# Preparing the recurrence's operands inside the projections instead of inside the recurrence

## The chip, the cores and the metric

The kernel runs on one core of a Trainium2 chip. The metric is the device time of one execution in microseconds (us). The engines are TensorE (PE in the profile, with PEld for its weight loads), VectorE (DVE), ScalarE (ACT), GpSimd (POOL) and SyncE (SP, which here only issues DMAs). Each engine works through its own queue in order and waits at an instruction whose inputs are not there yet.

## What is computed

One step of a two-layer decoder trunk in float32, for 1024 prompt tokens and for 64 sample tokens (8 sequences of 8) that share the weights. Layer 0 mixes with a convolution, layer 1 with RWKV-7; behind each mixer come cross-attention and a squared-ReLU MLP. The change touches the RWKV mixer alone:

```
xr, xw, xk, xv, xa, xg = (h + xx * mix[i] for i in range(6))        # xx = previous token - h
r, k, v = xr @ w_r, xk @ w_k, xv @ w_v
decay = exp(-exp(-softplus(-(w0 + tanh(xw @ w1) @ w2)) - 0.5))
a = sigmoid(a0 + (xa @ a1) @ a2);   g = sigmoid(xg @ g1) @ g2
kk = k * k_k;  kk = kk / max(norm(kk per head), eps);   k = k * (1 + (a - 1) * k_a)
for each token t, per head:                                         # state s is 64 x 64
    s = s * decay_t + (s @ -kk_t) (kk_t * a_t)^T + v_t k_t^T;   y_t = s @ r_t
y = groupnorm(y) * lnx_g + lnx_b + sum(r * k * r_k per head) * v
out = (y * g) @ w_o
```

The kernel works the loop over tokens in chunks of 64: inside a chunk it is a handful of matrix products and the inversion of a triangular matrix, and from chunk to chunk only the state goes on.

## The kernel before, in words

**Two streams.** The tokens are cut in two parts. Part A holds 512 prompt tokens, part B the other 512 and the 64 samples. Each part is a generator of work (`first()` and `second()`), and `pace` draws from both by a running estimate of their cost, so that in the program A's work stands between B's. A framework then schedules every engine's queue from its own model of durations. A's state goes into B, so B's recurrence comes after A's. The order in time is: A's projections beside B's first MLP, A's recurrence beside the end of that MLP and the start of B's projections, B's projections beside A's output product, B's recurrence beside A's second attention and MLP, and at the end B's second attention and MLP.

**Matrix products.** A weight tile `raw` (128 x 1024, 512 KB) comes by DMA, ScalarE rounds it to a high part (L96), VectorE makes the low part (L97), and `prod` does three matmuls for each piece (L142 to L144). `B_d<-u,wt` in a row is B's MLP, `A_d` and `B_d` are the streams' PSUM banks.

**Projections** (`projections`, from L729). `project(slot, ...)` makes r, k and v for eight row blocks m of 128 channels and two token tiles. Beside it run the small products: `hidden` makes the narrow side of the low-rank products and `lora` the wide one. All results go by a DMA from ScalarE's queue (`store`, L847) to six slots of `scr` in HBM. The last of them, `lora("a")`, stands behind the products of v.

**Shared splits.** The 24 weight tiles of r, k and v serve both parts. A writes the low part of each to `low` in HBM (`put`, L103), and B's `load` fetches it (L125) instead of making it.

**Recurrence** (`scan`, from L1088). For each chunk of 64 tokens three generators run side by side: `prep` of a chunk, `inverse` of the one before and `rest` (state, output, `finish`) of the one before that. `prep` loads all eight row blocks of the chunk as 128 x 512 tiles and makes from them `ar` (kk and r times the decay so far), `bk` (minus kk * a and k over the decay), the bonus `bon` and the norms `d32`: seven VectorE instructions of 512 columns (L1166 to L1258) and four small ones for the norms (L1212), three on ScalarE (L1168 to L1179), and six on GpSimd (L1189 to L1202). `finish` normalises the output with five GpSimd instructions of 512 columns (L1467 to L1471). A's recurrence has 8 chunks, B's has 8 and one of the samples: 17 in all.

## Time and profile before

| | us |
|---|---|
| three runs | 3832.77, 3834.26, 3837.16 |
| median | 3834.26 |
| the profiled execution | 3837.42 |
| its span, first to last instruction | 3835.7 |
| TensorE busy in the span | 3623.9 (94%) |
| VectorE, ScalarE, GpSimd busy | 2351.6, 1610.0, 660.7 |
| mean granted TensorE clock | 0.955 of 2.4 GHz |

The page says where the time is: TensorE is busy nearly throughout, at full clock in most slices. The exceptions are the convolution at the start, a stretch around 1900 us, and 2300 to 2800 us, where both the busy share and the granted clock fall. TensorE's busy time counts matmuls that overlap, and one at the lower of the two clock levels (1.2 GHz) is busy for longer, so busy time and clock are to be read together. All times below are counted from the start of the span.

### The profile page before, as it was taken

The numbers are of one execution on the slowest core, as the hardware profiler recorded it, in microseconds if no ns is written. First come the engines' busy times: TensorE is split into PE (matmuls) and PEld (weight loads), VectorE is DVE, ScalarE is ACT, GpSimd is POOL, SyncE is SP. The second block draws the span as 40 slices with busy tenths as digits, with TensorE's granted clock in tenths as the row PEclk, the third lists the DMA queues.
The fourth block names the chain that finished last, engine by engine and source line by source line (L and its number), as shares of the span: only waits on it lengthen the run. The fifth ranks groups of instructions, "written<-read, shape, count | busy, mean of one in ns | idle before, by whom it ended". The sixth has DMA issues, their size and how long they took to land.

```text
span 3835.7 us, 75763 instructions
## 1 busy us (share of the span) xinstructions
PE 3623.9 (94%) x30906; PEld 3369.6 (88%) x30906; DVE 2351.6 (61%) x4479; ACT 1610.0 (42%) x3190; POOL 660.7 (17%) x704
## 2 busy tenths in 40 slices
...
GB/s 226 132 53 129 80 67 106 102 114 170 153 90 83 126 151 152 159 138 112 85 88 109 232 254 146 111 93 70 54 113 120 114 120 197 121 72 83 83 83 64
DMA packets 333004, 456.03 MB, mean 119 GB/s; under 512 B 155248, under 2 KB 247664, under 8 KB 332656
## 3 DMA queue, kind: packets, MB, share of 16 engines
...
q14 instruction: 105, 0.86, 0.1%
...
## 4 chain that ended last, share of the span: by engine, by line
PE 77%; DVE 11%; ACT 4%; DMA 4%; issue 2%; POOL 1%; SPq 1%; ACTq 0%; DVEq 0%; POOLq 0%
PE B_d L142 11%; PE B_d L144 11%; PE B_d L143 11%; PE A_d L142 10%; PE A_d L143 9%; PE A_d L144 9%; PE A_d L362 3%; PE B_d L362 2%; DMA scr<-t_st 1%; SPq L1151 1%; PE A_hd L810 1%; PE A_d L442 1%; PE B_sa L608 1%; DVE wt L97 1%; PE B_sa L610 1%
## 5 line engine op out<-in xcount | busy, mean ns | idle before, releaser
L97 DVE TENSOR_TENSOR wt<-raw,wt 128x1024 fp32r<-128x1024 f32 x447 | 567.3, 1272 | 476.9 <-ACT wt L96 473.0
L96 ACT CAST wt<-raw 128x1024 fp32r<-128x1024 f32 x488 | 508.5, 1047 | 502.2 <-PE B_d L144 268.6
L142 PE MATMUL B_d<-hAB,wt 128*128 128x288 f32 (+1 forms) x2240 | 673.6, 303 | 15.4 <-ACT hAB L96 6.3
L143 PE MATMUL B_d<-hBB,wt 128*128 128x288 f32 (+1 forms) x2240 | 668.5, 299 | 1.2 <-DVE hBB L97 1.1
L144 PE MATMUL B_d<-hAB,wt 128*128 128x288 f32 (+1 forms) x2240 | 666.2, 298 | 0.3 <-DVE wt L97 0.3
L142 PE MATMUL A_d<-hAA,wt 128*128 128x256 f32 x2240 | 639.1, 288 | 15.0 <-ACT hAA L96 13.6
L143 PE MATMUL A_d<-hBA,wt 128*128 128x256 f32 x2240 | 642.4, 288 | 3.4 <-DVE hBA L97 3.4
L144 PE MATMUL A_d<-hAA,wt 128*128 128x256 f32 x2240 | 632.8, 285 | 2.5 <-POOL wt L97 2.2
L142 PEld LDWEIGHTS A_d<-hAA,wt 128*128 128x128 f32 x2240 | 429.0, 192 | 25.1 <-ACT hAA L96 16.8
L142 PEld LDWEIGHTS B_d<-hAB,wt 128*128 128x128 f32 x2240 | 425.4, 191 | 24.5 <-ACT hAB L96 7.5
L143 PEld LDWEIGHTS A_d<-hBA,wt 128*128 128x128 f32 x2240 | 430.2, 192 | 14.3 <-DVE hBA L97 5.6
L144 PEld LDWEIGHTS A_d<-hAA,wt 128*128 128x128 f32 x2240 | 428.6, 192 | 7.3 <-POOL wt L97 2.6
L143 PEld LDWEIGHTS B_d<-hBB,wt 128*128 128x128 f32 x2240 | 427.2, 191 | 6.5 <-DVE hBB L97 3.7
L711 POOL TENSOR_TENSOR t_sg<-t_ev 128x256 f32<-128x256 f32 (+1 forms) x256 | 185.5, 725 | 1418.2 <-ACT t_ev L709 1329.3
L144 PEld LDWEIGHTS B_d<-hAB,wt 128*128 128x128 f32 x2240 | 426.1, 190 | 2.3 <-issue 0.7
L142 PE MATMUL B_d<-u,wt 128*128 128x288 f32 x1024 | 307.1, 301 | 0.0
L144 PE MATMUL B_d<-u,wt 128*128 128x288 f32 x1024 | 303.3, 299 | 0.0
L143 PE MATMUL B_d<-u,wt 128*128 128x288 f32 x1024 | 303.3, 298 | 0.0
L143 PE MATMUL A_d<-u,wt 128*128 128x256 f32 x1024 | 288.2, 282 | 0.0
L144 PE MATMUL A_d<-u,wt 128*128 128x256 f32 x1024 | 288.2, 282 | 0.0
L142 PE MATMUL A_d<-u,wt 128*128 128x256 f32 x1024 | 287.4, 282 | 0.0
L97 DVE TENSOR_TENSOR u<-t_sg,u 128x256 fp32r<-128x256 f32 (+1 forms) x256 | 130.4, 510 | 149.9 <-ACT u L96 149.6
(401 smaller groups left out, 7068.8 us busy)
## 6 DMA issues: line engine op xcount, KB each, us to landing
raw<-in_mlp_up_dram SPq DMA_DIRECT2D x128, 512.0 KB, 3.6
raw<-in_mlp_dn_dram SPq DMA_DIRECT2D x128, 512.0 KB, 3.6
raw<-in_rw_w_dram SPq DMA_DIRECT2D x64, 512.0 KB, 4.2
ld<-scr SPq DMA_DIRECT2D x136, 128.0 KB, 3.2
wf<-in_w_in_dram SPq DMA_DIRECT2D x32, 512.0 KB, 4.0
raw<-in_xa_w_q_dram SPq DMA_DIRECT2D x32, 512.0 KB, 3.6
raw<-in_xa_w_o_dram SPq DMA_DIRECT2D x32, 512.0 KB, 3.6
raw<-in_ck_dram SPq DMA_DIRECT2D x32, 512.0 KB, 3.6
```

The source lines that it names most:

```text
L96: self.nc.scalar.copy(hi, src)
L97: (engine or self.nc.vector).tensor_tensor(lo, src, hi.bitcast(F32), SUB)
L142: self.nc.tensor.matmul(out, lhsT=wh, rhs=mh, start=(i == 0), stop=False)
L143: self.nc.tensor.matmul(out, lhsT=wh, rhs=ml, start=False, stop=False)
L144: self.nc.tensor.matmul(out, lhsT=wl, rhs=mh, start=False, stop=(i == last))
L362: nc.tensor.matmul(ps[:, :n], lhsT=wt[:, 0, k * P:k * P + P], rhs=h[:, k, t0:t0 + n], start=(k == 0), stop=(k == NC8 - 1))
L442: nc.tensor.matmul(ps[hs], lhsT=dg[:, q, h], rhs=two[h][:, 2 * q:2 * q + 512], start=(q == 0), stop=(q == pairs - 1))
L608: nc.tensor.matmul(out[:, h2], lhsT=wt.rearrange("p i t -> p (i t)"), rhs=moving[:, 0], start=start, stop=stop)
L610: nc.tensor.matmul(out[:64, h2], lhsT=wt[:, 0], rhs=moving[:, 1], start=False, stop=False)
L711: nc.gpsimd.tensor_mul(sg[:, :n], r[:, :n], r[:, :n])
L810: nc.tensor.matmul(ps[:, :n], lhsT=w1[:, m:m + P], rhs=hc[:, :n], start=(c == 0), stop=(c == NC8 - 1))
L1151: nc.sync.dma_start(out=dst[..., m * 64:m * 64 + 64], in_=scr[part][m][:, slots, t0:t0 + 64])
```

## The change

**A stage between projections and recurrence.** A new generator `stage(m, c0)` loads the six slots of one row block m for a pair of chunks (128 tokens; B also has a piece of 64 sample tokens), makes in place what `prep` made, and writes all six to `tls` in HBM. Its tiles `ld` (3 buffers in A, 2 in B), `kk`, `t1` and `ones` (one buffer each) live with the projections. It has 6 instructions on ScalarE, 9 on VectorE, 3 on GpSimd, 5 matmuls (four of them one column wide) and two DMAs. The part of `finish` that needs no output is made here too (bonus, bias and gate in slot v; scale times gate in slot g). There are 32 stages in A and 40 in B.

**Where it runs.** `project` of v draws one row block's stages after each of its six groups of the last token tile; the stages of the last two row blocks come after the projections. `hidden("a")` moves to the products of r and `lora("a")` to those of v, since a stage needs all six slots. The hidden tile that w and a shared becomes two.

**The recurrence** loads `ar` and `bk` ready from `tls`, copies the norms (one VectorE instruction of 16 columns) and does `finish` with three GpSimd instructions in place of five.

**The splits.** `low`, `put` and the `share` path go: B makes its 24 low parts itself.

The diff, cut to its core:

```diff
-weights = s.weights([(a["rw_w"][i, m], 1024, P, None, None, low[i][m]) for i in range(3) for m in range(NC8)])
+weights = s.weights([(a["rw_w"][i, m], 1024, P) for i in range(3) for m in range(NC8)])
...
+def stage(m, c0):
+    n, l, e, rs, at = (64, DSEQ, tail, ...) if c0 == 8 else (half, 64, ones, rst, slice(c0, c0 + 2))
+    ts = slice(64 * c0, 64 * c0 + n)
+    ld = hp.tile([P, 6, half], F32, tag="ld", name="ld", bufs=3 - part)
+    nc.sync.dma_start(out=ld[:, :, :n], in_=scr[part][m][:, :, ts])
+    w, r, ag, k, v, g = (ld[:, i, :n] for i in range(6))
+    kk, t1 = (hp.tile([P, half], F32, tag=x, name=x)[:, :n] for x in ("kk", "t1"))
+    nc.scalar.activation(kk, k, AF.Copy, scale=col("k_k", m))
+    nc.scalar.activation(t1, k, AF.Square, scale=col("k_k", m))
+    ps = s.bank()
+    ... nc.tensor.matmul(ps[hs, i:i + 1], lhsT=t1[hs, 64 * i:64 * i + 64], rhs=bones[hs, hs][:, :1], ...)
+    nc.vector.tensor_scalar_max(sums[part][:, m, c0:c0 + n // 64], ps[:, :n // 64], L2_MIN)
+    nc.vector.tensor_tensor_scan(out=w, data0=rs, data1=w, initial=0.0, op0=MUL, op1=ADD)
+    nc.scalar.activation(e[:, :, 1:], by(w, l), AF.Exp, scale=-DECAY)
+    nc.scalar.activation(w, w, AF.Exp, scale=DECAY)
+    nc.scalar.activation(t1, ag, AF.Identity, scale=col("k_a", m), bias=less[:, m:m + 1])
+    nc.vector.scalar_tensor_tensor(out=ag, in0=kk, scalar=-1.0, in1=ag, op0=MUL, op1=MUL)
+    nc.vector.scalar_tensor_tensor(out=t1, in0=t1, scalar=1.0, in1=k, op0=ADD, op1=MUL)
+    nc.gpsimd.tensor_tensor(ag, ag, w, MUL)
+    nc.vector.tensor_tensor(k, t1, w, MUL)
+    nc.vector.scalar_tensor_tensor(out=t1, in0=r, scalar=col("r_k", m), in1=t1, op0=MUL, op1=MUL)
+    nc.gpsimd.tensor_copy(ends[part][:, m, at], e[:, :, l])
+    nc.gpsimd.tensor_tensor(by(r, l), by(r, l), e[:, :, 1:], MUL)
+    nc.vector.tensor_tensor(by(w, l), by(kk, l), e[:, :, :l], MUL)
+    ps = s.bank()
+    nc.tensor.matmul(ps[:, :n], lhsT=bones, rhs=t1, start=True, stop=True)
+    nc.vector.tensor_tensor(v, v, ps[:, :n], MUL)
+    nc.vector.scalar_tensor_tensor(out=v, in0=v, scalar=col("lnx_b", m), in1=g, op0=ADD, op1=MUL)
+    nc.scalar.activation(g, g, AF.Copy, scale=col("lnx_g", m))
+    nc.sync.dma_start(out=tls[part][m][:, :, ts], in_=ld[:, :, :n])
...
+                if slot == 2 and tt == tiles[-1]:
+                    for _ in range(1 + 3 * len(pieces)):
+                        yield next(tiles_of, 0)
...
-yield from project(2, None, hidden(4, "a", [AF.Copy]), lora("gh", 5))
-s.put()
-yield from lora("a", 4)
+yield from project(2, None, lora("a", 2), lora("gh", 5))
+yield from tiles_of
...
-        L = ws
-        nc.vector.tensor_tensor_scan(out=L, data0=masks["rst"], data1=ws, initial=0.0, op0=MUL, op1=ADD)
...
+        load(ld, chunk, slice(0, 4))
+        ar, bk = ld[:, :, :2], ld[:, :, 2:]
...
-        nc.gpsimd.tensor_tensor(v3(y), v3(y), bvec("lnx_g"), MUL)
-        nc.gpsimd.tensor_tensor(v3(y), v3(y), bvec("lnx_b"), ADD)
-        nc.gpsimd.tensor_add(y, y, w["bon"])
-        nc.gpsimd.tensor_mul(y, y, gg)
+        nc.gpsimd.tensor_mul(v3(y), v3(y), gb[:, :, 1])
+        nc.gpsimd.tensor_add(v3(y), v3(y), gb[:, :, 0])
```

Three places of the engines' queues show the move. Line numbers of the kernel after differ a little: its products are L126 to L128 and its recurrence's lines stand two or three lower or higher.

**TensorE, between A's projections and its recurrence.** Before, B's MLP (`B_d<-u`) stands between and around the first matmuls of the recurrence (L1208, L1381):

```order
L143 MATMUL B_d<-u,wt 128x288
L1208 MATMUL p_pp<-c_bones,w 128x2 x4
L144 MATMUL B_d<-u,wt 128x288
L142 MATMUL B_d<-u,wt 128x288
L143 MATMUL B_d<-u,wt 128x288
L144 MATMUL B_d<-u,wt 128x288
L143 MATMUL B_d<-u,wt 128x288
L144 MATMUL B_d<-u,wt 128x288
L1381 MATMUL p_pz<-S,ar 64x64 x16
```

After, the last stages of A (L887 the norms, L906 the bonus) follow each other; eight such pairs stand ahead of these rows, and `hAB` behind them is the first product of B's projections:

```order
L887 MATMUL A_d<-c_bones,t_18462 64x1 x4
L906 MATMUL A_d<-t_18462,c_bones 128x128
L887 MATMUL A_d<-c_bones,t_18528 64x1 x4
L906 MATMUL A_d<-t_18528,c_bones 128x128
L887 MATMUL A_d<-c_bones,t_18558 64x1 x4
L906 MATMUL A_d<-t_18558,c_bones 128x128
L887 MATMUL A_d<-c_bones,t_18588 64x1 x4
L906 MATMUL A_d<-t_18588,c_bones 128x128
L1226 MATMUL p_pp<-ld 128x128 x2
L1379 MATMUL p_pz<-S,ld 64x64 x2
L126 MATMUL B_d<-hAB,wt 128x288 x2
```

B's MLP has ended ahead of A's last stages, and nothing of B stands between them.

**VectorE, at the start of B's projections** (`rest` is their first instruction). Before, it stands in the middle of A's recurrence, here between its lines for the inversion (`M`, `td`, `T`), the state `S` and the output `y`; `xB` is B's residual:

```order
L1313 STREAM_TRANSPOSE td<-M_20121 128x16x32
L1407 TENSOR_TENSOR S<-p_pz,S 128x512
L1322 STREAM_TRANSPOSE T_20125<-td 128x256
L1408 TENSOR_TENSOR S<-S,pcs 128x512
L725 TENSOR_TENSOR xB_169<-xB_169,B_d 128x288
L769 TENSOR_SCALAR rest<-vec 128x48
L1456 SCALAR_TENSOR_TENSOR y<-p_pz,y 128x512
L1228 TENSOR_TENSOR Aak<-p_pp,c_strict_p 64x4x64
```

After, it stands one row behind A's last stage (L889 to L909 are a stage's lines), and A's recurrence begins with it:

```order
L889 TENSOR_SCALAR sums_105<-A_d 128x2
L896 SCALAR_TENSOR_TENSOR ld<-kk,ld 128x128
L897 SCALAR_TENSOR_TENSOR t_18588<-t_18588,ld 128x128
L899 TENSOR_TENSOR ld<-t_18588,ld 128x128
L900 SCALAR_TENSOR_TENSOR t_18588<-ld,vec,t_18588 128x128
L903 TENSOR_TENSOR ld<-kk,ones 128x128
L907 TENSOR_TENSOR ld<-ld,A_d 128x128
L909 SCALAR_TENSOR_TENSOR ld<-ld,vec 128x128
L1274 STREAM_TRANSPOSE dt<-d_18650 128x32
L756 TENSOR_SCALAR rest<-vec 128x48
```

So B's norm, which stood beside A's recurrence, now stands ahead of A's last stages, and B's mixing behind them.

**TensorE, A's second attention and MLP** (L558, L546 after: transposed softmax tiles). Before, the attention stands among the matmuls of B's recurrence:

```order
L1400 MATMUL p_half<-Aq,UV 64x64 x8
L1406 MATMUL p_pz<-UV,BK 64x64
L558 MATMUL A_d<-c_ident,e 128x128 x4
L1455 MATMUL p_pz<-y,c_bones 128x512
L142 MATMUL A_d<-pr,wt 128x256
```

After, it stands among B's stages, and B's recurrence stands among A's MLP (`A_d<-u`), here some 1600 rows later:

```order
L887 MATMUL B_d<-c_bones,t_27047 64x1 x2
L906 MATMUL B_d<-t_27047,c_bones 128x64
L546 MATMUL A_d<-c_ident,e 128x128 x4
L887 MATMUL B_d<-c_bones,t_27075 64x1 x4
L126 MATMUL A_d<-pr,wt 128x256
...
L1325 MATMUL p_half<-T_30500,dgz 32x16 x13
L128 MATMUL A_d<-u,wt 128x256
L126 MATMUL A_d<-u,wt 128x256
L1237 MATMUL p_pp<-c_ident,v 128x128 x4
```

## Rows read from the trace of the kernel before

**Rows 1.** Busy time by stage (engine busy us, count), granted clock, DMA share, GB/s:
```profile
core 0: us, PE busy (x) PEld busy (x) DVE busy (x) ACT busy (x) POOL busy (x), PEclk, DMA share, GB/s
1305.00:1734.00 429.00, 428.77 (x3300) 425.17 (x3299) 206.19 (x401) 198.74 (x431) 29.66 (x46) 1.00 0.49 153
1734.00:2140.00 406.00, 364.94 (x4759) 313.71 (x4759) 320.54 (x709) 225.01 (x448) 125.07 (x113) 0.90 0.38 105
2140.00:2391.00 251.00, 232.16 (x1599) 217.94 (x1598) 103.62 (x230) 125.37 (x275) 2.92 (x9) 0.95 0.70 218
2391.00:2865.00 474.00, 429.08 (x5517) 362.05 (x5516) 367.67 (x753) 226.25 (x453) 163.87 (x129) 0.88 0.31 81
2865.00:3366.00 501.00, 500.08 (x4103) 498.11 (x4102) 273.38 (x449) 207.91 (x370) 96.15 (x110) 1.00 0.43 136
```
**Rows 2.** The same view, single stretches of 100 us:
```profile
300.00:400.00 100.00, 95.48 (x564) 80.00 (x565) 96.16 (x166) 31.92 (x63) 7.62 (x12) 0.95 0.40 125
400.00:500.00 100.00, 96.52 (x569) 75.70 (x568) 96.31 (x154) 26.30 (x61) 15.41 (x10) 1.00 0.27 80
1800.00:1900.00 100.00, 91.77 (x1341) 79.54 (x1341) 77.18 (x163) 51.73 (x103) 36.42 (x33) 0.92 0.30 72
1900.00:2000.00 100.00, 80.98 (x1149) 65.39 (x1149) 89.69 (x227) 52.91 (x111) 34.65 (x35) 0.76 0.35 92
2000.00:2100.00 100.00, 94.97 (x1387) 80.10 (x1386) 72.68 (x159) 59.84 (x119) 24.33 (x20) 0.93 0.37 110
2600.00:2700.00 100.00, 97.28 (x1436) 82.86 (x1436) 83.03 (x164) 50.59 (x95) 35.02 (x27) 0.93 0.32 81
```
**Rows 3.** Chain of waits, 1880 to 2020 us, its shares by line:
```profile
by line: DVE xB L738 8.4%; DVE hBB L97 5.5%; DVE M L1304 4.7%; DVE t_dl L783 4.7%; issue 4.6%; DVE ld L1171 3.9%; SPq L1151 3.7%; PE B_d L142 3.6%; PE B_d L144 3.3%; PE B_d L143 3.3%; DVE hc L783 2.8%; DVE w L1192 2.5%; DVE Aak L1228 2.4%; 
```
**Rows 4.** VectorE groups of the recurrence, 1734 to 2140 us (busy us, mean ns):
```profile
L1171 DVE TENSOR_TENSOR_SCAN ld<-rst,ld 128x512 f32<-128x512 f32 x8 | 12.3, 1532 | 0.0
L1192 DVE SCALAR_TENSOR_TENSOR w<-ld,vec 128x512 f32<-128x512 f32 x8 | 8.2, 1029 | 0.0
L1194 DVE SCALAR_TENSOR_TENSOR ld<-w,ld 128x512 f32<-128x512 f32 x8 | 7.7, 964 | 0.0
L1197 DVE SCALAR_TENSOR_TENSOR w<-w,ld 128x512 f32<-128x512 f32 x8 | 6.4, 804 | 0.0
L1166 DVE TENSOR_TENSOR w<-ld,vec 128x512 f32<-128x512 f32 x8 | 5.6, 699 | 7.3 <-DMA gg<-scr 3.0 <-DMA v<-scr 2.5 <-issue 1.8
L1203 DVE TENSOR_TENSOR w<-w 128x512 f32<-128x512 f32 x8 | 5.5, 682 | 0.2 <-PE p_pp L1208 0.2
L1258 DVE TENSOR_TENSOR bon<-v,p_pp 128x512 f32<-128x512 f32 x8 | 5.4, 680 | 5.3 <-PE p_pp L1256 5.3
L1212 DVE TENSOR_SCALAR d<-p_pp 64x8 f32<-64x8 f32 x32 | 5.2, 163 | 0.8 <-PE p_pp L1208 0.5
```
**Rows 5.** Single lines, whole run: duration min/median/max in ns:
```profile
L786 DVE SCALAR_TENSOR_TENSOR t_dl<-before,vec,t_dl x24: 267/278/1286, 1995.2 to 2229.2; 128x64 f32<-128x64 f32 x24
L841 DVE TENSOR_TENSOR w<-raw,w x48: 283/290/420, 1337.9 to 2366.7; 128x128 fp32r<-128x128 f32 x48
L836 ACT CAST w<-raw x64: 280/294/309, 1336.7 to 2366.2; 128x128 fp32r<-128x128 f32 x48, 96x128 fp32r<-96x128 f32 x16
L1171 DVE TENSOR_TENSOR_SCAN ld<-rst,ld x17: 1191/1223/2290, 1743.9 to 2740.3; 128x512 f32<-128x512 f32 x17
```
**Rows 6.** Costliest groups of the page: the split of one weight tile:
```profile
L97 DVE TENSOR_TENSOR wt<-raw,wt 128x1024 fp32r<-128x1024 f32 x447 | 567.3, 1272 | 476.9 <-ACT wt L96 473.0
```
**Rows 7.** ScalarE group of a table load, 1734 to 2140 us:
```profile
L1463 ACT ACT_TABLE_LOAD x8 | 10.3, 1283 | 0.1
```
**Rows 8.** DMA issues: count, KB each, median us from issue to landing:
```profile
ld<-scr SPq DMA_DIRECT2D x136, 128.0 KB, 3.2
low<-wt SPq DMA_DIRECT2D x24, 512.0 KB, 3.0
wt<-low SPq DMA_DIRECT2D x24, 512.0 KB, 4.6
```
**Rows 9.** TensorE groups of the recurrence, 1734 to 2140 us:
```profile
L1208 PE MATMUL p_pp<-c_bones,w 128*128 128x2 f32 x64 | 10.7, 286 | 0.0
L1256 PE MATMUL p_pp<-w,c_bones 128*128 128x512 f32 x16 | 12.7, 886 | 0.0
L1381 PE MATMUL p_pz<-S,ar 64*64 64x64 f32 x256 | 12.8, 235 | 0.7 <-ACT rs L1463 0.7
L1245 PE MATMUL p_pp<-c_ident,bk 128*128 128x128 f32 x64 | 11.6, 318 | 5.5 <-DVE Aq L1229 5.1 <-ACT UV L1237 0.2
```

154 lines of the change are left out of this document (58 added, 96 removed).

## The prediction

> **What bounds the kernel now.** I read the page first: TensorE is busy 94% of the span, so time can only come from where it stands still or runs at the lower clock. The view by stages [rows 1] shows where that is. I call lost time the span less TensorE's busy time, plus the span times what the clock lacks to 1. A's projections (1305 to 1734 us) lose nothing: 428.77 busy of 429 at clock 1.00. A's recurrence (1734 to 2140) loses 41 + 0.10 x 406 = 82 us. B's projections (2140 to 2391) lose 19 + 0.05 x 251 = 31. B's recurrence (2391 to 2865) loses 45 + 0.12 x 474 = 102. Behind it nothing is lost again. The sum is 215 us, and the stages hold 324 + 220 + 372 = 916 us of TensorE's work beside it. Idle time at the lower clock is counted twice here, so 215 is a little high.
>
> What goes with the loss is VectorE's load. Per us of TensorE's work VectorE is busy 0.48 in A's projections, and 0.99 in both recurrences (320.54 / 324 and 367.67 / 372). Single stretches [rows 2] give the scale: at 0.83 (2000 to 2100) 12 us of 100 are lost, at 0.92 (1800 to 1900 and 2600 to 2700) 16 and 10, at 1.57 (1900 to 2000) 43. The worst stretch is B's norm and mixing beside A's recurrence; its chain of waits [rows 3] is led by VectorE lines of both. But 300 to 500 us, in the convolution, has VectorE at 96% and loses only 3.5 to 9.5 of 100: a full VectorE alone does little harm where TensorE has work that does not hang on it.
>
> **What the recurrence loses.** Per chunk the removed VectorE groups [rows 4] are (12.3 + 8.2 + 7.7 + 6.4 + 5.6 + 5.5 + 5.4 + 5.2) / 8 = 7.0 us; a copy of 16 columns comes in, priced as L1212 at 0.16. Over 17 chunks that is 117 us less. GpSimd loses all of `prep` and two of five instructions of `finish`, on an engine busy 125 and 164 us there [rows 1]; it is off the path, but it slows VectorE (below).
>
> **What the projections gain.** A stage's VectorE work: three two-operand instructions as the 128-column L841 at 0.29, four with a scalar between the 64-column L786 (0.278) and the 512-column L1194 (0.964) at 0.34, the running sum at 0.45 (a quarter of L1171's 1.223 and some 0.15 that does not shrink), the maximum at 0.16: 2.8 us [rows 4, 5]. 64 full stages and 8 short ones at 2.2 make 200 us. B's 24 own splits at 1.272 [rows 6] are 30. So VectorE has 113 us more in all; quarter-size pieces cost more than their share. ScalarE gets 6 x 0.294 x 72 = 127 us [rows 5] and, by the new order, 35 more table loads, since the stages' Exp alternates with `lora`'s Sigmoid: 35 x 1.283 = 45 us [rows 7], against three 512-column instructions less per chunk.
>
> The table load's row has 1.283 us each and 0.1 us of idle time ahead of eight of them. The Trainium skill ("ScalarE: Activation LUTs", What ACT_TABLE_LOAD costs) adds a drain of about 1.38 us to each switch. By that the 35 would be an estimated 93 us; this trace does not show the drain, and the sum goes by the row.
>
> TensorE: out go 17/8 x (10.7 + 12.7) = 50 us of L1208 and L1256. In come 272 one-column matmuls, each two records of at most L1381's 12.8 / 256, so 27, and 72 of 128 columns as L1245's records of 11.6 / 64, two each, so 26 [rows 9]. That is +3 us. The DMAs: a stage moves 393 KB in and out, 72 times; `low` goes, 24 writes and 24 reads of 512 KB [rows 8]. SP's queue gets 144 issues and loses 48. An `ld` load waits there for the buffer's last store, and weight loads of both streams queue behind it. Ring and raw buffers hold several tiles ahead, so I cost that at nothing in the sum; if the cover is gone it is part of the first rival.
>
> **What moves.** The order puts B's MLP to its end and B's norm beside A's projections, A's last twelve stages behind them with nothing between, A's recurrence beside B's projections, B's stages beside A's second attention, and B's recurrence beside A's MLP. Counting matmul columns along the order, about 70 us of the 916 move into A's projections; 275 lie beside A's recurrence, 275 beside B's products of v and stages, 295 beside B's recurrence. I price the lost time of each place:
> - A's first 20 stages run beside the last third of its projections (143 us): VectorE 69 + 20 x 2.8 = 125, or 0.88, where TensorE has B's MLP to do. By 300 to 500 us [rows 2] that loses 5 to 14; I take 8. Now it is 0.
> - A's last twelve stages: `kk` and `t1` have one buffer, so a stage's six ScalarE instructions (1.8) and four of VectorE (1.3) follow each other, with some 0.5 for the matmul and the hand-overs: 3.6 us. Three `ld` buffers with 3.2 to load and 3.0 to store [rows 8] allow about the same. 12 x 3.6 = 43, then a store and a load before the recurrence can start, 6, and a lower clock behind the pause as at 1900 to 2000 us, 9: 58. Bounds 40 and 75.
> - A's recurrence beside B's projections: of VectorE's 320.5 now [rows 1] go 8 x 7.0 = 56 and some 36 for the end of B's MLP and B's norm, which move ahead; 16 own splits bring 20. That is 248, or 0.90. 13% of 275 is 36; bounds 5% and 19%, 14 and 52.
> - B's stages beside A's attention: 40 stages are 112. Of the rest B's projections now have 103.6 [rows 1]; some 90 of A's attention and norm come in, which stand in B's recurrence now, and some 45 go ahead with B's products of r and k: 149. Eight own splits are 10. The sum of 271 is 0.98. 18% is 50; bounds 3.5% and 27% (B's recurrence now), 10 and 75.
> - B's recurrence beside A's MLP: of VectorE's 367.7 now [rows 1] go 9 x 7.0 = 63 and the 90 of A's attention and norm, and some 60 of A's MLP come in: 275, or 0.93. 14% is 41; bounds 5% and 27%, 15 and 80.
>
> The sum is 8 + 58 + 36 + 50 + 41 = 193 against 215: 22 less, and 3 more of TensorE's work, so 19 us gained. The profiled execution (3837.42, span 3835.7) would become 3818, and against the median of the runs, 3.2 lower, it is 3815.
>
> **Rivals.** (1) Slower: TensorE's queue is in order, and each of B's 40 stages stands in it twice, with A's work between. The order gives a stage 275 / 40 = 6.9 us of TensorE's work. B has two `ld` buffers, so load, work and store come to (3.2 + 3.6 + 3.0) / 2 = 4.9 when nothing disturbs. For it: ScalarE and VectorE are shared with A's softmax there, the loads share SP's queue and a DMA busy 0.70 at 218 GB/s [rows 1]. At 9.5 us a stage the place loses 40 x 2.6 = 104 in place of 50, and the kernel takes 3869. It decides from 8.6 us on (50 + 19 = 40 x 1.7). (2) No change: B's stages lose 69 and all cancels, 3834; VectorE's 113 us more speak for it. (3) A larger gain: a recurrence beside dense products loses only 5%, as at 300 to 500 us, in both: 14 + 15 in place of 36 + 41, so 3767. For it: L1171 takes 1.19 at least and 2.29 at most [rows 5], and the longest are in stretches where GpSimd works. Of eleven GpSimd instructions a chunk three are left.
>
> The Trainium skill ("GPSIMD Engine Reference", Key points) says that GpSimd shares its SBUF interfaces with VectorE and that instructions with two SBUF inputs contend. By that rule the rest of the recurrence's VectorE work gets shorter too, which is rival 3; the stages, though, bring 216 GpSimd instructions into the projections.
>
> **How the numbers follow.** The forecast, 3815 with its own range of 3800 to 3826, has 0.38; rival 1 has 0.33, rival 2 0.14, rival 3 0.15. Differences under 0.2% (7.7 us) cannot be told from no change here. Faster is 0.38 + 0.15 = 0.53, same 0.14, slower 0.33. The range runs from rival 3 to rival 1, 3767 to 3869; what lies beyond them is under 0.2.
>
> **What would show it.** The twelve stages of A as a gap of TensorE of 40 to 60 us, with a lower clock behind it. Stages of B at 5 to 7 us each, with TensorE's waits for `t1` under 50 us in all; over 8.6 means rival 1. VectorE under 30 us per chunk of 64 in the recurrences, and lost time beside A's MLP near 14%. The prediction is wrong if the sum of lost time in these stages is not 180 to 205 us, above all if A's projections lose more than 20, or if the waits move to weight tiles behind SP's queue.

## The result and the profile after

The kernel after takes 4072.65 us (median of 4 runs, 4067.76 to 4083.57) beside 3835.71 for the kernel before in the same comparison. The ratio is 1.062, with a 95% interval of 1.060 to 1.065: 237 us slower, where 19 us faster was forecast and 3869 was the upper end of the range. The profiled execution has a span of 4081.7 us, 246 more than before. TensorE is busy 3737.4 us (92%), VectorE 2389.3, ScalarE 1761.3, GpSimd 570.0.

The view by stages of the kernel after, to be read beside [rows 1] (columns as there). The cuts are: A's stages beside B's MLP, A's last stages, A's recurrence, B's stages, B's recurrence in two pieces, and what comes behind it, with B alone from 3610 us on:

```profile
core 0: us, PE busy (x) PEld busy (x) DVE busy (x) ACT busy (x) POOL busy (x), PEclk, DMA share, GB/s
1305.00:1842.00 537.00, 519.88 (x3992) 509.94 (x3990) 289.03 (x636) 269.52 (x588) 59.03 (x109) 0.98 0.45 138
1842.00:1943.00 101.00, 39.38 (x274) 32.41 (x272) 48.17 (x169) 38.23 (x105) 19.10 (x58) 0.62 0.49 145
1943.00:2313.00 370.00, 345.49 (x4474) 290.94 (x4475) 252.05 (x628) 232.85 (x488) 28.93 (x23) 0.87 0.41 107
2313.00:2766.00 453.00, 361.02 (x2508) 330.61 (x2507) 243.26 (x656) 234.13 (x541) 65.91 (x138) 0.83 0.55 170
2766.00:3083.00 317.00, 312.39 (x3875) 267.73 (x3877) 200.20 (x469) 129.32 (x256) 47.13 (x48) 0.89 0.39 101
3083.00:3167.00 84.00, 65.85 (x1206) 50.50 (x1205) 42.14 (x97) 39.42 (x76) 11.62 (x10) 0.72 0.17 38
3167.00:3610.00 443.00, 421.21 (x3402) 417.72 (x3402) 230.93 (x386) 187.88 (x335) 94.64 (x101) 0.97 0.44 138
3610.00:4081.00 471.00, 443.64 (x3281) 439.61 (x3279) 208.90 (x411) 136.75 (x243) 43.74 (x66) 0.97 0.26 80
```

Lost time is taken as in the prediction, the span less TensorE's busy time, plus the span times what the clock lacks to 1. In the second row, for one, it is (101 - 39.38) + 0.38 x 101 = 100.

| place | before | forecast | after |
|---|---|---|---|
| A's stages beside B's MLP, to 1842 | 0 | 8 | 28 |
| A's last stages, to 1943 | | 58 | 100 |
| A's recurrence, to 2313 | 82 | 36 | 73 |
| B's stages (before: B's projections), to 2766 | 31 | 50 | 169 |
| B's recurrence, to 3167 | 102 | 41 | 81 |
| behind it | 54 | (54) | 77 |
| sum | 269 | 193 + (54) | 528 |

Up to 1303 us both kernels are alike. The prediction had no term for what stands behind B's recurrence: it wrote that nothing is lost there, which is right to 3366 us and misses 54 us behind that. The table carries these 54 over as its forecast. The sums differ by 259, the spans by 246: idle time at the lower clock is counted twice, and TensorE's own work changed too. So the recurrences gained, but 9 and 21 us where 46 and 61 were forecast, and the stages lost 297 where 116 were forecast.

The stages' pace stands in the first and last start of the four one-column matmuls that each has (view of line L887, durations in ns). A's 32 stages start (1938.1 - 1622.8) / 31 = 10.2 us apart on average, B's 40 start (2753.9 - 2320.2) / 39 = 11.1 apart. A's mean hides two paces: the first twenty are held apart by the products that the program puts between them, and the last twelve start (1937.7 - 1879.5) / 11 = 5.3 us apart:

```profile
L887 PE MATMUL B_d<-c_bones,t x288: 193/214/264, 2320.2 to 2753.9; 64*64 64x1 f32 x144
L887 PE MATMUL A_d<-c_bones,t x256: 193/214/263, 1622.8 to 1938.1; 64*64 64x1 f32 x128
```

What TensorE stood still for at the stages is in the groups of L887 (norms) and L906 (bonus). The last columns are the idle time ahead and who ended it: 45.0 + 17.2 + 8.6 + 19.9 + 12.0 = 103 us.

```profile
L906 PE MATMUL A_d<-t,c_bones 128*128 128x128 f32 x64 | 18.3, 377 | 45.0 <-DVE t L900 45.0
L887 PE MATMUL B_d<-c_bones,t 64*64 64x1 f32 x288 | 17.6, 218 | 19.9 <-ACT t L883 16.5 <-ACT t_st L849 3.4
L906 PE MATMUL B_d<-t,c_bones 128*128 128x128 f32 x64 | 16.3, 343 | 17.2 <-DVE t L900 17.2
L887 PE MATMUL A_d<-c_bones,t 64*64 64x1 f32 x256 | 15.0, 217 | 12.0 <-ACT t L883 12.0
L906 PE MATMUL B_d<-t,c_bones 128*128 128x64 f32 x16 | 3.8, 331 | 8.6 <-DVE t L900 8.6
```

ScalarE and VectorE stood still too, at the first instruction of a stage that reads its load (`kk`, L882, and the running sum, L891):

```profile
L882 ACT ACTIVATE kk<-ld,vec 128x128 f32<-128x128 f32 x64 | 25.7, 401 | 132.9 <-DMA ld<-scr 72.9 <-DVE ld L903 59.5 <-ACT t_st L849 0.4
```

```profile
L891 DVE TENSOR_TENSOR_SCAN ld<-rst,ld 128x128 f32<-128x128 f32 x64 | 27.1, 424 | 155.7 <-DMA ld<-scr 150.2 <-ACT t_st L849 5.5
```

133 and 156 us. Of ScalarE's 133, 73 ended with the load and 59.5 with L903 of VectorE, the last reader of `kk`, which has one buffer. The chain of waits between 2640 and 2760 us, shares by line, is two thirds transfers:

```profile
by line: DMA ld<-scr 35.0%; DMA tls<-ld 33.2%; ACT ld L910 3.0%; issue 2.6%; DVE ld L891 2.0%; ACT kk L882 1.9%; DVE ld L909 1.7%; PE A_d L127 1.7%; ACT t L883 1.6%; DVE e L539 1.1%; PE B_d L906 1.0%; DVE wt L96 0.9%; DVE hBA L96 0.9%; ACT 
```

A stage's load, its work and its store follow each other there, and hardly two stages overlap.

### The profile page after: what moved, and what is told of

Its sections match the earlier page's. It is cut to its first block, busy times and chain, and to the rows that moved or that the text cites. A ratio compares the mean times of both kernels' runs of the same rounds, so it can differ in the third digit from the quotient of the medians.

```text
span 4081.7 us, 77967 instructions
## 1 busy us (share of the span) xinstructions
PE 3737.4 (92%) x31424; PEld 3454.6 (85%) x31424; DVE 2389.3 (59%) x4981; ACT 1761.3 (43%) x3606; POOL 570.0 (14%) x786
## 4 chain that ended last, share of the span: by engine, by line
PE 68%; DMA 12%; DVE 9%; ACT 7%; issue 3%; POOL 1%; SPq 1%; ACTq 0%; DVEq 0%; POOLq 0%
PE B_d L126 9%; PE B_d L128 9%; PE B_d L127 9%; PE A_d L127 8%; PE A_d L128 8%; PE A_d L126 8%; DMA ld<-scr 4%; DMA tls<-ld 4%; PE A_d L350 3%; PE B_d L350 2%; PE p_pp L1226 2%; DVE wt L96 1%; ACT wt L95 1%; DMA yl<-yg 1%; DMA raw<-in_g_dram 1%
## 5 line engine op out<-in xcount | busy, mean ns | idle before, releaser
L96 DVE TENSOR_TENSOR wt<-raw,wt 128x1024 fp32r<-128x1024 f32 x471 | 592.1, 1260 | 452.2 <-ACT wt L95 449.9
L95 ACT CAST wt<-raw 128x1024 fp32r<-128x1024 f32 x512 | 533.1, 1046 | 509.8 <-PE B_d L128 234.0
L126 PE MATMUL B_d<-hAB,wt 128*128 128x288 f32 (+1 forms) x2240 | 679.6, 305 | 37.6 <-ACT hAB L95 25.4
L128 PE MATMUL B_d<-hAB,wt 128*128 128x288 f32 (+1 forms) x2240 | 672.6, 301 | 0.3 <-DVE wt L96 0.3
L126 PE MATMUL A_d<-hAA,wt 128*128 128x256 f32 x2240 | 646.5, 291 | 22.2 <-ACT hAA L95 14.3
L128 PE MATMUL A_d<-hAA,wt 128*128 128x256 f32 x2240 | 636.9, 287 | 5.3 <-DVE wt L96 3.3
L126 PEld LDWEIGHTS B_d<-hAB,wt 128*128 128x128 f32 x2240 | 430.7, 193 | 49.7 <-ACT hAB L95 28.7
L126 PEld LDWEIGHTS A_d<-hAA,wt 128*128 128x128 f32 x2240 | 433.2, 194 | 35.7 <-ACT hAA L95 18.9
L127 PEld LDWEIGHTS A_d<-hBA,wt 128*128 128x128 f32 x2240 | 433.3, 194 | 12.6 <-DVE hBA L96 4.6
L128 PEld LDWEIGHTS A_d<-hAA,wt 128*128 128x128 f32 x2240 | 432.4, 194 | 11.2 <-DVE wt L96 4.3
L128 PEld LDWEIGHTS B_d<-hAB,wt 128*128 128x128 f32 x2240 | 430.6, 193 | 3.1 <-issue 0.7
L126 PE MATMUL B_d<-u,wt 128*128 128x288 f32 x1024 | 305.0, 299 | 2.8 <-ACT u L95 2.3
L128 PE MATMUL B_d<-u,wt 128*128 128x288 f32 x1024 | 302.9, 298 | 0.3 <-DVE wt L96 0.3
L127 PE MATMUL A_d<-u,wt 128*128 128x256 f32 x1024 | 292.3, 286 | 0.0
L128 PE MATMUL A_d<-u,wt 128*128 128x256 f32 x1024 | 291.0, 285 | 0.0
L126 PE MATMUL A_d<-u,wt 128*128 128x256 f32 x1024 | 289.6, 285 | 0.0
```

Source lines behind the costliest of these rows:

```text
L95: self.nc.scalar.copy(hi, src)
L96: (engine or self.nc.vector).tensor_tensor(lo, src, hi.bitcast(F32), SUB)
L126: self.nc.tensor.matmul(out, lhsT=wh, rhs=mh, start=(i == 0), stop=False)
L127: self.nc.tensor.matmul(out, lhsT=wh, rhs=ml, start=False, stop=False)
L128: self.nc.tensor.matmul(out, lhsT=wl, rhs=mh, start=False, stop=(i == last))
```

## Experiments

Two questions were open. What did the stages cost, and through what? And why did the recurrences gain so little, with VectorE's work out of them? Times are compared with 4073 us for the kernel after and with the kernel before as run beside each. The kernel before came out between 3832 and 3842 us in these comparisons, and most of the kernels here ran two to five times, so a difference of some 10 us from 4073 tells little. The pace of B's stages is told by the issue times of their 40 stores (kernel after: 11.1 us). Lost time is told by place, as in the table; for B the stages' place and the recurrence behind it are added, since several runs only moved time from one to the other (kernel after: 169 + 81 = 250; before: 133).

### The premise alone

```diff
-        kk = w512()
-        nc.vector.tensor_tensor(v3(kk), v3(k), bvec("k_k"), MUL)
+        kk = k
...
-        nc.vector.tensor_tensor_scan(out=L, data0=masks["rst"], data1=ws, initial=0.0, op0=MUL, op1=ADD)
...
-        nc.scalar.activation(En, L, AF.Exp, scale=DECAY)
+        nc.scalar.activation(En, L, AF.Copy, scale=0.0)
...
-        nc.vector.scalar_tensor_tensor(out=bp, in0=kk, scalar=-1.0, in1=ag, op0=MUL, op1=MUL)
```

(L1192, L1197 and L1203 go in the same way.)

> The kernel before, with six of the seven VectorE instructions of 512 columns in prep left out (L1166, L1171, L1192, L1194, L1197, L1203: 5.7 us a chunk, 97 us in all) and nothing moved; the output is not the reference's. One Exp of ScalarE becomes a Copy with scale 0. It measures the premise of the prediction by itself. Premise (VectorE's load of 0.99 per us of TensorE's work sets the time lost in the recurrences; at 0.85 some 13.5% are lost): A's recurrence loses 44 in place of 82, B's 50 in place of 102, and the time falls by 90 us to about 3745. Rival (the recurrence's chain over all engines and TensorE's clock set it, VectorE's load does not): the time falls by less than 30 us, to no less than 3805.

Measured: 3802.53 us, ratio 0.992 (0.990 to 0.993), 32 us faster. The two recurrences of this kernel:

```profile
1742.00:2089.00 347.00, 328.37 (x4544) 282.05 (x4543) 260.40 (x634) 198.12 (x403) 103.84 (x102) 0.91 0.38 105
2367.00:2789.00 422.00, 388.25 (x5135) 321.03 (x5135) 291.95 (x666) 207.46 (x424) 134.93 (x115) 0.87 0.30 81
```

A's loses 18.6 + 0.09 x 347 = 50 in place of 82, B's 33.8 + 0.13 x 422 = 89 in place of 102. Per us of TensorE's work VectorE is busy 0.88 in both, and one loses 17% of it, the other 27%. The forecast's scale would give some 13% for both. In the kernel after the same figures are 0.85 and 25% for A, 0.76 and 25% for B. So VectorE's load alone does not set what a recurrence loses. The premise came out in part: A's recurrence fell nearly to the 44 us that it asks for, B's stayed far from its 50, and the 32 us stand just outside the rival's bound of 30. In all it was worth a third of the 90 us that the prediction's scale gives for it.

### The stages emptied

```diff
-            ld = hp.tile([P, 6, half], F32, tag="ld", name="ld", bufs=3 - part)
-            nc.sync.dma_start(out=ld[:, :, :n], in_=scr[part][m][:, :, ts])
...
-            nc.sync.dma_start(out=tls[part][m][:, :, ts], in_=ld[:, :, :n])
+            nc.sync.dma_start(out=tls[part][m][:, :, ts], in_=zero[:, :, :n])
```

> The kernel after with its 72 stages emptied: each only stores a constant tile of zeros to the slots (one DMA, no load, no engine instruction); norms and decay ends are constants, so the output is not the reference's. The recurrence reads its operands ready-made as in the kernel after. Theory 1 (the stages themselves are the loss: chains of load, work and store that TensorE's queue waits for): the 24 + 111 + 164 us lost at the stages' places fall to about 40 and 30 us of TensorE's work goes, so about 3780 us, below the kernel before. Theory 2 (the loss is in the order: the recurrences no longer have enough other work beside them): the 63 + 114 us lost in the recurrences stay and more is added, so 3880 us or more.

Measured: 3888.37 us, ratio 1.014 (1.010 to 1.019): 184 less than the kernel after, and still above the kernel before. By its number that is theory 2, but part of it is the experiment's own. The stores have nothing to wait for, so they came in two bursts, A's within 49 us and B's within 52. In the first and third row DMA stands at 0.90, and 22 and 30 us are lost; the third lies inside A's recurrence. In the first, by the trace's releasers, ScalarE waits 13.5 and 6.9 us for such a store to land, and TensorE behind it. In the third, TensorE's waits name no transfer, so that the burst costs those 30 us is not shown. Apart from that, B's recurrence loses 36 + 88 = 124, more than before, with its operands ready and no stage ahead of it:

```profile
1350.00:1400.00 50.00, 36.19 (x248) 35.58 (x247) 15.81 (x27) 15.25 (x33) 4.84 (x5) 0.83 0.90 262
1744.00:2137.00 393.00, 368.15 (x4566) 308.61 (x4566) 247.13 (x615) 194.44 (x394) 43.12 (x49) 0.87 0.46 124
1976.00:2029.00 53.00, 40.85 (x481) 32.53 (x480) 38.40 (x101) 26.53 (x59) 7.50 (x13) 0.67 0.90 260
2381.00:2869.00 488.00, 452.25 (x5138) 362.92 (x5136) 283.85 (x678) 205.97 (x425) 56.56 (x46) 0.82 0.30 82
```

```diff
+            if part:
+                for _ in range(3):
+                    yield .2
+                nc.sync.dma_start(out=tls[part][m][:, :, ts], in_=zero[:, :, :n])
+                return
```

> The kernel after with only B's 40 stages emptied in that way (A's stay; the output is not the reference's). Theory 1 (the loss is in the stages, at 11 us each in B for 6.9 us of cover): the place loses about 30 in place of 164 and 15 us of TensorE's work goes, so about 3925 us. Theory 2 (the order): the time falls by less than 60 us, to no less than 4010.

Measured: 3962.52 us, 110 less than the kernel after; B's two places lose 24 + 103 = 127 in place of 250. Theory 1 holds for B's stages (24 of the 169 are left). B's recurrence loses 22 more than in the kernel after and A's 18 more (91), and the time misses theory 1's 3925 by 38.

### A stage taken apart

The next five kernels keep the place, the count and the load and store of the stages and leave out work between them.

```diff
-            nc.scalar.activation(kk, k, AF.Copy, scale=col("k_k", m))
...
+            nc.scalar.activation(ld[:, :, :n], ld[:, :, :n], AF.Copy, scale=0.0)
             nc.sync.dma_start(out=tls[part][m][:, :, ts], in_=ld[:, :, :n])
```

> The kernel after with each stage cut to its load, one ScalarE instruction over the whole tile and its store (no VectorE, GpSimd or TensorE instruction in a stage; the output is not the reference's). If the two transfers of 393 KB and SyncE's queue set the pace (a store that waits keeps the weight loads behind it), the time stays above 3950 us. If the chain of the 18 instructions on four engines sets it, the pace of B's stages falls from 11 us to under 7 and the time comes within 30 us of the kernel with emptied stages.

Measured: 3859.71 us, 213 less than the kernel after, ratio to before 1.009 (1.005 to 1.013). By the issue times of the stores B's pace is 5.6 us. A's places lose 24 + 70 = 94 (after: 201, before: 82), B's 70 + 78 = 148. Loads, stores and SyncE's queue are the small part.

```diff
-                    nc.tensor.matmul(ps[hs, i:i + 1], lhsT=t1[hs, 64 * i:64 * i + 64], rhs=bones[hs, hs][:, :1],
-                                     start=True, stop=True)
-            nc.vector.tensor_scalar_max(sums[part][:, m, c0:c0 + n // 64], ps[:, :n // 64], L2_MIN)
...
-            nc.tensor.matmul(ps[:, :n], lhsT=bones, rhs=t1, start=True, stop=True)
-            nc.vector.tensor_tensor(v, v, ps[:, :n], MUL)
+            nc.vector.tensor_tensor(v, v, t1, MUL)
```

> The kernel after with the five TensorE matmuls of each stage left out, and the one VectorE maximum that reads the first four (the norms are a constant, the bonus takes t1 in place of its sum over the head; the output is not the reference's). Everything else of a stage stays: loads, stores, ScalarE, VectorE, GpSimd. TensorE then never waits for a stage. Theory 1 (the stages cost because each stands twice in TensorE's in-order queue, with A's products behind it): B's stages lose near the 70 us that they lose with transfers alone, in place of 169, A's 40 or less in place of 134, and the time is 3900 or below. Rival (a stage's 18 instructions slow the splits and the softmax that TensorE's products need, through ScalarE and VectorE): B's place still loses over 130, and the time stays above 3980.

Measured: 3941.25 us, 131 less, between the 3900 of theory 1 and the 3980 of the rival. Not all of it is waiting: TensorE's busy time falls by 73 us (3737 to 3664) and its idle time by 67 (344 to 277). The matmuls' own rows add up to 71 us busy (L887 and L906 above), where the prediction had 53. The stages' places of A and of B:

```profile
1303.00:1821.00 518.00, 486.15 (x3606) 474.22 (x3604) 304.91 (x696) 304.75 (x671) 74.73 (x147) 0.98 0.53 159
2183.00:2585.00 402.00, 308.96 (x1937) 282.44 (x1935) 224.79 (x577) 250.63 (x576) 65.58 (x135) 0.85 0.65 194
```

A's loses 31.9 + 10.4 = 42 in place of 128: theory 1 holds there, nearly to its 40. B's still loses 93 + 60 = 153 of its 169, as the rival has it, though B's pace is 8.0 us now and the place 51 us shorter. What TensorE waits for there is A's softmax, the evacuations of B's projections and the splits (waits in that window: total, times, longest), and ScalarE in turn for the stages' loads:

```profile
PE A_d L548 <- DVE e L541: 21.7, 3, 10.8
PE B_d L126 <- ACT t_st L851: 15.1, 9, 4.6
PE A_d L126 <- ACT wt L95: 7.3, 6, 1.8
```

```profile
ACT kk L884 <- DMA ld<-scr: 51.8, 23, 5.4
```

```diff
-            nc.scalar.activation(kk, k, AF.Copy, scale=col("k_k", m))
-            nc.scalar.activation(t1, k, AF.Square, scale=col("k_k", m))
+            nc.scalar.activation(k, k, AF.Copy, scale=0.0)
+            nc.scalar.activation(ag, k, AF.Square, scale=col("k_k", m))
...
-            nc.vector.tensor_tensor_scan(out=w, data0=rs, data1=w, initial=0.0, op0=MUL, op1=ADD)
...
-            nc.gpsimd.tensor_tensor(ag, ag, w, MUL)
```

> The kernel after with each stage cut to its load, its six ScalarE instructions (two of them Exp) and its store; no VectorE, GpSimd or TensorE instruction, so that the output is not the reference's. With transfers alone (one ScalarE instruction) the time was 3860 and B's place lost 70 us, with everything but the matmuls 3941 and 153. If ScalarE's work and its table loads, ahead of the splits and evacuations in its queue, are what the stages cost beyond their transfers, this comes to 3920 or above; if VectorE's are, to 3880 or below.

Measured: 3939.87 us; B's two places lose 103 + 105 = 208, at a pace of 6.4 us.

```diff
-            nc.scalar.activation(kk, k, AF.Copy, scale=col("k_k", m))
...
-            nc.vector.scalar_tensor_tensor(out=ag, in0=kk, scalar=-1.0, in1=ag, op0=MUL, op1=MUL)
+            nc.vector.scalar_tensor_tensor(out=ag, in0=k, scalar=0.0, in1=ag, op0=MUL, op1=MUL)
...
-            nc.gpsimd.tensor_tensor(ag, ag, w, MUL)
```

> The counterpart: each stage cut to its load, eight VectorE instructions of the same sizes and its store; no ScalarE, GpSimd or TensorE instruction, output not the reference's. If VectorE's work is what costs, 3920 or above; if ScalarE's is, near the 3860 of the transfers alone. If both stay below 3890, it is the chain from engine to engine that costs, not the work of either.

Measured: 3913.75 us; 99 + 92 = 191 at 6.6 us. Beside the 3860 with transfers alone, ScalarE's work costs 80 us and VectorE's 54, and both with GpSimd's cost 81 (3941). So the two do not add up: either engine's part alone makes two thirds or more of what they make together with GpSimd's. The reading that one of the two is to blame falls. That it is their place ahead of the products' splits and evacuations in the two queues agrees with the waits listed above, but no run changes that place alone.

```diff
-            nc.scalar.activation(e[:, :, 1:], by(w, l), AF.Exp, scale=-DECAY)
-            nc.scalar.activation(w, w, AF.Exp, scale=DECAY)
+            nc.scalar.activation(e[:, :, 1:], by(w, l), AF.Copy, scale=0.01)
+            nc.scalar.activation(w, w, AF.Copy, scale=0.0)
```

> The kernel after with the two Exp of each stage replaced by Copy (same tiles and sizes; the output is not the reference's). The 35 table loads that the change brings (38 before, 73 after, 1.28 us each) go. If they cost their own time on TensorE's path, the time falls by 30 to 45 us, to about 4035; by the prediction, which counted them as ScalarE time beside other work, it falls by under 15.

Measured: 4068.73 us, 4 less, which cannot be told from no change. The whole trace has 66 table loads, where the kernel after has 91 and the kernel before 56, so 25 of the 35 went (32 us of ScalarE's time). These cost nothing that shows. In the kernel after a load in a stage takes 1283 ns, with 0.3 us of idle time ahead of 15:

```profile
L892 ACT ACT_TABLE_LOAD x15 | 19.2, 1283 | 0.3
```

The Trainium skill ("ScalarE: Activation LUTs", What ACT_TABLE_LOAD costs) has 1.28 us for the load, which this row confirms, and a drain of 1.38 beside it, which neither the row nor this run shows.

### Buffers, queues and cover

```diff
-            kk, t1 = (hp.tile([P, half], F32, tag=x, name=x)[:, :n] for x in ("kk", "t1"))
+            kk, t1 = (hp.tile([P, half], F32, tag=x, name=x, bufs=2)[:, :n] for x in ("kk", "t1"))
```

> The kernel after with two buffers in place of one for kk and t1 in both parts; nothing is left out. If the single buffers keep a stage from starting before the one ahead is done (A's last stages stand 5.2 us apart), these come to about 4 us apart and B's to 8 or 9, and the time falls by 50 to 100 us, to about 4000. If the two ld buffers of B and the place of the stage's matmuls in TensorE's queue set the pace, it falls by under 20 us.

Measured: 4062.12 us, 11 less. By the starts of L906 A's last eight stages came to 4.7 us apart from 5.2, and A's stages lose 62 + 37 = 99 in place of 128, B's two places 163 + 82 = 245. The rival holds.

```diff
-            nc.sync.dma_start(out=tls[part][m][:, :, ts], in_=ld[:, :, :n])
+            nc.scalar.dma_start(out=tls[part][m][:, :, ts], in_=ld[:, :, :n])
```

> The kernel after with the stages' stores issued by ScalarE instead of SyncE; nothing is left out. If a store that waits in SyncE's queue for its stage keeps the next load and the weight tiles behind it (SyncE waits 97 us for L910 and 82 for the stores to land, between 2320 and 2760 us), the pace of B's stages falls below 9 us and the time by 40 us or more, to 4030 or below. If the chain of load, work and store in two buffers sets the pace, it stays within 20 us of 4073; if ScalarE's queue now waits for VectorE, it gets slower.

Measured: 4087.18 us, 15 more; B's pace 11.4. The stores' place in SyncE's queue is not what sets it; the loads stayed there.

```diff
-            ld = hp.tile([P, 6, half], F32, tag="ld", name="ld", bufs=3 - part)
+            ld = hp.tile([P, 6, half], F32, tag="ld", name="ld", bufs=3)
```

> The kernel after with three ld buffers in B, as A has them; to make room B's mixing temporary (dl) and the tile of lora's raw weights have one buffer in place of two, and the samples' reset row shares a tile. Nothing is left out. In the kernel after, between 2313 and 2766 us, ScalarE stands 77 us at L882 and VectorE 78 us at L891, both for a load of ld, with the splits of A's products behind them in their queues. Theory 1 (two buffers make each load wait for the store of two stages before, and that sets B's 11 us): the pace falls to 8 us or less, these waits to under 30 us, the place loses 110 or less in place of 169, and the time falls by 40 us or more, to 4030 or below. Rival (the place in TensorE's queue and the work of a stage set the pace): the pace stays above 10 us and the time within 20 us of 4073.

Measured: 4092.62 us, 20 more; B's pace 10.4. ScalarE's wait for loads went, and others came in its place, ScalarE for VectorE and VectorE for the load (waits between 2300 and 2782 us: total, times, longest):

```profile
ACT kk L882 <- DVE ld L903: 32.3, 19, 5.0
ACT ld L910 <- DVE ld L909: 28.3, 17, 4.6
```

```profile
DVE ld L891 <- DMA ld<-scr: 97.4, 38, 7.0
```

```diff
-            ld = hp.tile([P, 6, half], F32, tag="ld", name="ld", bufs=3 - part)
+            ld = hp.tile([P, 6, half], F32, tag="ld", name="ld", bufs=3)
...
-            nc.tensor.matmul(ps[:, :n], lhsT=bones, rhs=t1, start=True, stop=True)
```

> Both at once: three ld buffers in B as in the run with them alone, and the stages without their matmuls (and the maximum that reads them), so that the output is not the reference's. Without matmuls alone the time was 3941 and B's place still lost 153 us at a pace of 8.0 us. If what was left there is the wait for loads in ScalarE's and VectorE's queues, the place now loses under 100 us and the time is 3900 or below, near the 3860 of the stages with transfers alone. If it is the work of the stages on ScalarE and VectorE, or the want of other products beside them, the place loses over 130 and the time stays above 3925.

Measured: 3927.81 us, 13 less than without the matmuls alone, at a pace of 6.8 us; B's stages' place loses 148, of 411 us. The pace has the 6.9 us that the order leaves a stage, and the place loses as much as before, so the pace is not what costs here. That is the second reading, and this run does not part its two halves. The stages with transfers alone stand beside the same work of A (memory, output product, attention and norm) and lose 70 there, so about half of the 148 comes with the stages' work on ScalarE and VectorE.

```diff
-OFFSET = 5.0
+OFFSET = 75.0
```

> The kernel after with one number changed, so that B's stream starts later (OFFSET 75 in place of 5): by the order, part of B's MLP then stands between and behind A's last stages. Theory 1 (A's last twelve stages lose 111 us because nothing else stands in TensorE's queue there): the place loses 50 or less, and the time falls by 50 to 80 us, to about 4010. Rival (the stage's chain slows whatever stands beside it): B's MLP is stretched instead and the time falls by under 20 us.

Measured: 4127.00 us, 54 more. The places are A's stages, B's stages, B's recurrence and what comes behind:

```profile
1303.00:1934.00 631.00, 576.25 (x4426) 561.29 (x4424) 315.52 (x748) 300.07 (x662) 80.59 (x171) 0.95 0.46 137
2257.00:2861.00 604.00, 517.49 (x3847) 490.30 (x3847) 323.48 (x799) 301.95 (x690) 81.76 (x162) 0.89 0.53 161
2861.00:3251.00 390.00, 358.76 (x4756) 292.94 (x4755) 223.33 (x530) 155.43 (x305) 53.02 (x48) 0.80 0.32 82
3251.00:4123.00 872.00, 807.26 (x6056) 794.26 (x6056) 423.51 (x746) 301.79 (x536) 125.46 (x153) 0.95 0.34 105
```

A's stages lose 54.8 + 31.6 = 86 in place of 128: less, as theory 1 has it, but the time rose, as neither reading has it. B's two places lose 153 + 109 = 262, and what is behind them 108 in place of 77. A's recurrence has 82, the first 1303 us 23 more. Work that covers one chain is missing beside the next.

### The order inside ScalarE's and VectorE's queues

In the order of VectorE's queue the next stage's running sum (L891) stands ahead of the last instructions of the stage at hand (L907, L909), and so on ScalarE's with L882 and L883 ahead of L910:

```
2683 L903 TENSOR_TENSOR ld<-kk,ones 128x128
2684 L891 SCALAR_TENSOR_TENSOR ld<-rst,ld 128x128
2685 L907 TENSOR_TENSOR ld<-ld,B_d 128x128
2686 L96 TENSOR_TENSOR pr<-A_d,pr 128x512
2687 L909 SCALAR_TENSOR_TENSOR ld<-ld,vec 128x128
```

```diff
-            nc.vector.tensor_tensor_scan(out=w, data0=rs, data1=w, initial=0.0, op0=MUL, op1=ADD)
+            nc.vector.tensor_tensor_scan(out=sc[:, :n], data0=rs, data1=w, initial=0.0, op0=MUL, op1=ADD)
...
             nc.scalar.activation(g, g, AF.Copy, scale=col("lnx_g", m))
+            nc.vector.tensor_copy(sc[:, :1], v[:, :1])
+            nc.scalar.copy(kk[:, :1], g[:, :1])
```

> The kernel after, complete, with a forced order: the running sum goes to a tile of its own with one buffer, and one column of that tile and of kk is written once more behind a stage's last VectorE and ScalarE instruction. So a stage's first instructions (L882, L891), which wait for its load, can no longer stand in the queues ahead of the last ones (L907, L909, L910) of the stage before, as they do in the kernel after. Theory 1c (that order makes each store wait for the next stage's load, and each load waits for a store: 3.1 + 3.8 us and some 3 of work, one stage at a time, are B's 10 us, whatever the buffers): the pace of B's stages falls to 7 us or less, the place loses 90 or less in place of 169, the time falls by 70 us or more, to 4000 or below. Rival (the work of a stage and the place of its matmuls in TensorE's queue set the pace): the pace stays above 9 us and the time within 25 us of 4073.

Measured: 4040.81 us, 32 less. A's stages lose 111, B's two places 148 + 95 = 243; the pace is 10.7. By the pace the rival holds, by the time neither does.

```diff
             nc.scalar.copy(kk[:, :1], g[:, :1])
+            nc.scalar.copy(t1[:, :1], g[:, :1])
```

> As in the run before, with one column of t1 written once more too, so that L884 (the Square into t1, L883 in the kernel after), which in that run still stood ahead of the last ScalarE instruction of the stage before, cannot. Nothing else changes. With L882 and L891 held back alone, the pace in B fell from 11.1 to 10.7 (median 9.4 to 8.9) and the time to 4041; ScalarE still stood 41 us at this one instruction for loads. Theory 1c: with the last of the three held back the pace falls to 7 us or less and the time by 40 us or more, to 4000 or below. Rival (the work and TensorE's queue): within 20 us of 4041.

Measured: 4124.27 us, 83 more than the run before. The pace is 12.6. The waits for loads are gone (VectorE's is 12 us, ScalarE's no longer among the longest), the stages' place of B loses 140 of 534 us, and B's recurrence, with less beside it, 150. Theory 1c falls as the cause of the pace. What couples the stages is not settled.

The paces of these runs are not to be compared by themselves, since a pace holds the other work that the order puts between two stages. The place has 534 - 140 = 394 us of TensorE's work here, 461 - 148 = 313 in the run before, 482 - 168 = 314 with three buffers, and 453 - 169 = 284 in the kernel after. Lost time over 40 stages is the better measure: 4.2 us in the kernel after and with three buffers, 3.7 and 3.5 in the two runs of this section.

### The two small parts alone

```diff
-weights = s.weights([(a["rw_w"][i, m], 1024, P, None, None, low[i][m]) for i in range(3) for m in range(NC8)])
+weights = s.weights([(a["rw_w"][i, m], 1024, P) for i in range(3) for m in range(NC8)])
```

> The kernel before with one part of the change alone: B makes its 24 low parts itself (24 splits of 1.27 us on VectorE, the 24 writes and 24 reads of 512 KB go). By the prediction's sum this is 30 us of VectorE's time beside TensorE's work, hidden: within 6 us of the kernel before. If the reads of the low parts were what B's projections wait for, it is 10 us or more faster; if VectorE is the bound there, 10 us or more slower.

Measured: 3850.89 us, ratio 1.0043 (1.0027 to 1.0059): 16 us slower.

```diff
-        yield from project(0, 2, hidden(1, "w", [AF.Tanh]))
+        yield from project(0, 2, hidden(1, "w", [AF.Tanh]), hidden(4, "a", [AF.Copy]))
...
-        yield from project(2, None, hidden(4, "a", [AF.Copy]), lora("gh", 5))
+        yield from project(2, None, lora("a", 4), lora("gh", 5))
         s.put()
-        yield from lora("a", 4)
```

> The kernel before with another part of the change alone: the narrow and the wide side of a's low-rank product move to the products of r and of v, with a tile of their own (no stage, nothing else). By the prediction this costs nothing: within 6 us of the kernel before. If the last products of lora standing alone at the end of A's projections are part of what is lost at the recurrence's start, it is 5 to 15 us faster.

Measured: 3857.81 us, ratio 1.0051 (1.0034 to 1.0068): 20 us slower. Neither edit adds work to TensorE's queue. In both it is a recurrence that loses more (own splits: A 96, B 117; moved products: A 82, B 127; before: 82 and 102). B's is shown here, first with its own splits, then with the products moved:

```profile
2397.00:2857.00 460.00, 402.42 (x5282) 334.98 (x5282) 357.41 (x736) 215.23 (x431) 146.01 (x115) 0.87 0.29 79
```

```profile
2383.00:2837.00 454.00, 395.43 (x5159) 327.42 (x5160) 351.69 (x749) 213.75 (x438) 142.89 (x113) 0.85 0.30 82
```

```diff
+weights = s.weights([(a["rw_w"][i, m], 1024, P) for i in range(3) for m in range(NC8)])
...
+        yield from project(0, 2, hidden(1, "w", [AF.Tanh]), hidden(4, "a", [AF.Copy]))
...
+        yield from project(2, None, lora("a", 4), lora("gh", 5))
```

> The kernel before with both small parts of the change, B's own splits and the moved low-rank products of a, and nothing else. Alone they cost 15 and 20 us where the prediction had nothing. If they add up, this is 30 to 40 us slower than the kernel before, so about 3870; if both only shift which products stand beside the recurrences, one can make up for the other and it is 10 to 25 us slower.

Measured: 3828.50 us (9 runs) beside 3839.03 (12 runs), ratio 0.998 (0.997 to 0.999): 8 us faster. So the two costs do not add up. An edit that adds nothing to TensorE's queue and gives the scheduler another order moves this kernel by up to 20 us. The runs show no mechanism behind it, and the 32 us of the premise are known no better than that. This kernel, complete and with both small parts of the change without the stages, is the fastest of the complete ones.

## Why the prediction was wrong

**The stages' price (the failed step).** The prediction took the lost time beside B's stages from VectorE's load (0.98, so 18% and 50 us) and A's last twelve stages from the length of their own instructions (3.6 us each, 58 us in all). These two terms measured 169 and 100, above the bound of 75 that each had. The five places together lost 451 us for the 193 of the sum; of the 258 between them B's stages are 119, A's last stages 42, A's first stages 20 and the two recurrences 77. VectorE's load is not what did it: beside B's stages it was 243 / 284 = 0.86 per us of TensorE's work, less than forecast.

The work itself was sized better. VectorE's instructions of a full stage take 0.443 + 0.424 + 0.368 + 0.365 + 0.318 + 0.283 + 0.283 + 0.280 + 0.155 = 2.92 us (forecast 2.8), ScalarE's 2.29 (forecast 1.76), load and store 3.9 and 3.3 (forecast 3.2 and 3.0), all 344 matmuls 71 (forecast 53). What the sum had at nothing is that these instructions stand in four in-order queues with another stream's work between them, and that this stream's work stands behind them. The runs without parts of a stage show what the parts were worth: 131 us through the matmuls (73 of TensorE's busy time among them), 81 through the work on the other engines (80 with ScalarE's alone, 54 with VectorE's), and 24 for all that remains against before, transfers and reordering less what the recurrences gained.

**Rival 1 had the outcome, and a mechanism that holds in part.** The kernel is slower, B's pace is 11.1 where it decides from 8.6, and the place lost 169. Its formula gives 40 x (11.1 - 6.9) = 168, but that is bookkeeping: span less work, with the measured pace put in. It named TensorE's queue, in which each of B's stages stands twice. Without these matmuls B's place still lost 153, so this is the small part there; it holds at A's stages (42 in place of 128). The sharing of ScalarE and VectorE with A's softmax, which it names as a point for it, fits B's place better. Its time fell short by its pace of 9.5 and by leaving all other places at the forecast's values. Its buffer sum (two `ld` buffers) was no part of it: three gained nothing.

**A's last twelve stages.** The pause and the lower clock were forecast; the size was not (100, bounds 40 and 75). From 1842 to 1879.5 us stand B's norm and the last products of v and `lora`, with 14.0 + 8.6 = 23 us lost that the term did not have. From there to the recurrence's first matmul at 1947 the twelve stages, 5.3 us apart and not 3.6, and the wait for the load lose 51.1 + 31.7 = 83 at a clock of 0.53. Without the matmuls the whole place of A's stages loses 42.

**The recurrences.** "What goes with the loss is VectorE's load" does not hold as the measure it was used for. VectorE's busy time fell as forecast (A's recurrence 252 for 248, B's 242 for 275), and the lost share of TensorE's work stayed at 25% in both (before 25% and 27%). The scale was read from stretches of 100 us as VectorE's time per us of TensorE's work, and that work is the stretch less the lost time. Where time is lost the ratio rises by itself. Idle time did fall (A's recurrence 41 to 25, B's 45 to 23), but what was lost to the clock did not (41 to 48, 57 to 58).

**Rival 3** (a recurrence beside dense products loses 5%) was not the case. Between 2766 and 3083 us A's MLP stands beside B's recurrence, and 39 us are lost, 35 of them by the clock; that is 14% of TensorE's work there, the forecast's figure. That was luck: the forecast had it from a VectorE load of 0.93, and the load there was 200 / 278 = 0.72. The other 42 of the 81 went between 3083 and 3167, where no product of A stands in the order, as none starts in the trace. So 41 fits the part that has cover, and the further step that failed is that the whole recurrence would have it.

**Costed at nothing.** SyncE's queue: right as far as it was tested (another queue for the stores gains nothing). The table loads as time beside other work: right for the 25 that could be taken out, and 35 more was exact (91 in the whole trace in place of 56). The own splits and the moved products: each cost some 16 to 20 us alone and gained 8 together, so "nothing" was right in no single case, and no sum over instructions could have given it. Behind B's recurrence another 23 us went (77 in place of 54), which the prediction did not look at. TensorE has one wait of 18.4 us there, for the high part that B's output product starts with (`hAB`, L95).

The prediction's own signs of being wrong came true: the lost time is 451 and not 180 to 205, A's projections lose 28 where 20 was the limit, and B's pace is over 8.6. One sign came out as forecast: TensorE's waits at the matmuls of B's stages are 17.2 + 8.6 + 19.9 = 46 us, under the 50, in a place that lost 169. That too says that TensorE's queue is the small part there.

**What stays open.** Why 4.2 us are lost at each of B's stages beside 7.1 us of TensorE's work (284 / 40), where ScalarE and VectorE work 2 to 3 us on it: buffers, the stores' queue and the order inside two queues were tried one at a time, and none gave more than 32 us. Another cut of the stages (fewer and larger ones, or another place for B's) was not tried. And why TensorE's clock falls inside the recurrences whatever VectorE does.
